# A hybrid attention and delta-rule layer on one core: TensorE's order written out through the merges

## The chip, the cores and the metric

The kernel runs on one core of a Trainium2 chip. The metric is device time of one launch in microseconds, the median of several runs. Besides, one execution was recorded by the hardware profiler; all traces below are of that kind.

## The reference, cut to what matters

One layer over 1024 latent tokens (16 rows of 64 columns) and 256 context tokens, width 1024, float32. Half of the mixing width is neighbourhood attention (8 heads of 64), the other half a bidirectional chunked gated DeltaNet (4 heads of 128), in chunks of which each needs the inverse of a unit lower triangular matrix.

```python
h = rmsnorm(x, g_pre) * (1 + scale) + shift;  hc = the same of ctx
na_q, na_k, na_v, na_z, g_qkv, g_z, g_b, g_a = split(h @ w_in)
o_na = neighborhood_attention(...)                # window 8 x 16, plus all context keys
q, k, v = gdn_qkv(g_qkv, conv_w)                  # centred conv, silu, l2norm, rotary
a = where(pos[:, None] > pos[None, :], (k * beta) @ k.T * decay, 0)
t_inv = triangular_solve(eye + a, eye)            # per chunk, head and direction
u = t_inv @ (v * beta);  w = t_inv @ (k * beta * exp(gc))
state, o = scan(...)                              # forward and backward over the chunks
y = concat([o_na * silu(na_z), rmsnorm(o_g) * silu(g_z)]) @ w_out
return x + gate * rmsnorm(y, g_post)
```

## The kernel before, in words

The kernel uses chunks of 128 tokens: 10 chunks (2 of context, 8 latent) for each of 4 heads and 2 directions, so 80 matrices `pm` of 128x128 whose inverses are needed. A float32 product of the projections is made of three products of rounded parts (`hh`, `hl` for the activations, `wh`, `wl` for the weights), in `mm_chan` and `mm_tok`.

Phases: `phase0` (modulation, first projections), `phase2` (projections, convolutions and the scan's front for the four heads, with other projections as filling), `phase_a2` (the last projections, the inverses, the loads for attention), `phase_b` (attention and scan by turns, then the output projection). In `phase_b` TensorE's order is written out: `pe(r)` orders each product behind the last one on the queue, without a semaphore. Before `phase_b` the order of every engine is set by Tile's scheduler, which gives the instructions of each engine an order from their place in the program, a priority (`tc.high_priority(offset)` moves instructions ahead by that many places) and a modelled time; the engines then run them in that order.

The projections left to `phase_a2` are those of the generator `projections`: two pairs of value tiles (264 columns a product), then queries, keys and gates of the attention pairs 2 and 3 (512 or 256 columns a product). A result in `pz` goes through ACT and DVE to `st_z` and by DMA to `z_dram` (line 557).

The inverses are built in two steps. `inv_groups`/`inv_blocks` invert the 320 diagonal blocks of 32x32 on DVE (lines 1078 and 1081), 120 blocks at a time; groups 0 and 1 are done in `phase2`, group 2 (80 blocks, tiles `ab_vv` and `tb_qh`) in `phase_a2` by the generator `blocks`, which then loads the masks and, when three heads are merged, the inputs of attention's pair 0 (`na_load`: `kk`, `qh`, `ql`, `gt`, `vv`). `inv_merge` then joins the blocks of one head into 64x64 and 128x128 inverses. It is a generator of stages, which `MERGES` calls by head and letter:
- l: load `pm` of the head into `pmf` and the inverted blocks into `vl`
- t: DVE transposes (lines 1114 to 1116) to `vd` and `ld`, ACT copies into `tm[0]`
- z: TensorE products `pm` by blocks (line 1128), ACT copies to `zt`; then ACT and POOL copies into `xo` and `tm[1]` (line 1137)
- u: TensorE (line 1147), DVE into `tm` and `xo` (line 1152)
- w: TensorE, the 64x64 level (line 1161), ACT copies to `z2`
- e: TensorE (lines 1167 and 1169), two halves of five chunks each in two PSUM buffers `tb`, DVE into `tm` (lines 1171 and 1172), DMA to `tm_dram` (line 1174)

`tm[0]` is one of two buffers by turns (`tms[h % 2]`), `tm[1]` is `tms[2]` for all heads, and so is `xo`. PSUM has three banks `ta`, two `tb` and three `pj` here. In `phase0`, `self.after` puts the first query product of one group of rows behind the last of the modulation's small products (line 310) on TensorE's queue. In `phase_a2` a step of the projections alternates with three steps of `blocks` and three of `merges`, all merge stages 200 places ahead. The scan's loads (`delta_load`: `tm`, `v`, `kt`, `kq`, `qe`, line 156) go to a pool that takes the memory of `wp` (weights, `st_z`) and `hp` (`hh`, `hl`). SP's queue issues nearly all DMAs, in one order; the weights' loads are on ACT's queue. In the scan, line 1232 (POOL) makes `kd` from `kt`, line 1260 (TensorE) is a step's first product here and line 1271 uses `kd`.

Of the kernel before, what the change touches and what calls it, by code (L numbers as in the profile page):

```python
# [11 lines left out]
F32 = mybir.dt.float32  # L12
# [125 lines left out]
MERGES = "0l 0t 1l 0z 0u 1t 0w 2l 0e 1z 1u 2t 1w 3l 1e 2z 2u 3t 2w 2e 3z 3u 3w 3e"  # L138
# [3 lines left out]
class K:  # L142
    def __init__(self, tc, I, out, dbg=None):
        self.tc, self.nc, self.I, self.out = tc, tc.nc, I, out
        self.dbg = dbg or {}
        self.na_first = None
        self.gm = {}
        self.gate = self.after = None
# [306 lines left out]
    def mm_chan(self, ps, w, hh, hl, t0, n, perm=False, ks=range(KC)):  # L455
        nc = self.nc
        his, los = w
        for k in ks:
# [4 lines left out]
            r = nc.tensor.matmul(ps, wh, xh, start=(k == 0), stop=False)  # L463
            if self.after:
                self.order(r, self.after)
                self.after = None
            nc.tensor.matmul(ps, wh, xl, start=False, stop=False)  # L467
            nc.tensor.matmul(ps, wl, xh, start=False, stop=(k == KC - 1))  # L468

    def mm_tok(self, ps, w, c0, n, xsel, ks=range(KC)):  # L470
        nc = self.nc
        his, los = w
        for k in ks:
            wh, wl = his[k][:, c0:c0 + n], los[k][:, c0:c0 + n]
            xh, xl = xsel(k)
            nc.tensor.matmul(ps, xh, wh, start=(k == 0), stop=False)  # L476
            nc.tensor.matmul(ps, xl, wh, start=False, stop=False)  # L477
            nc.tensor.matmul(ps, xh, wl, start=False, stop=(k == KC - 1))  # L478
# [610 lines left out]
    def inv_merge(self, g3, ps, h):  # L1089
        nc = self.nc  # L1090
        pm = []
        for d in range(2):
            pool, tag = (g3, f"pm{d}") if h % 2 else (self.pf, f"kk{d}")
            pm.append(pool.tile([P, 10, P], F32, name=f"pmf{h}_{d}", tag=tag))
            nc.sync.dma_start(pm[d][0:96], self.pm_dram[h][0:96, d])
        if h == 0:

            self.vls = [self.pf.tile([P, S], F32, name=f"vl{i}", tag=f"q{c}") for i, c in enumerate(("l0", "h1"))]
            self.tms = [g3.tile([P, 10, P], F32, name=f"tm{i}") for i in range(3)]
            self.xo = g3.tile([P, 10, 64], F32, name="xo")  # L1100
# [7 lines left out]

        xo = self.xo
        tm = [self.tms[h % 2], self.tms[2]]  # L1110
        yield
        vx = self.pf.tile([P, S], F32, name=f"vx{h}", tag="ql1")
# [10 lines left out]
        for d in range(2):  # L1123
            pz = ps.tile([P, 10, 32], F32, name=f"tz{h}_{d}", tag="ta", bufs=3)
            for t in range(10):
                for b in (0, 2):
                    s1, s2 = slice(32 * b, 32 * b + 32), slice(32 * b + 32, 32 * b + 64)
                    nc.tensor.matmul(pz[s2, t, :], pm[d][s1, t, s2], ld[s1, d, t, :], start=True, stop=True,
                                     tile_position=(32 * b, 32 * b + 32))
# [10 lines left out]
        for d in range(2):  # L1140
            pu = ps.tile([P, 10, 32], F32, name=f"tu{h}_{d}", tag="tb", bufs=2)
            where = [(r, r + c - 1) for r in (1, 3) for c in (0, 1) if (r, c) != ((3, 1), (1, 0))[d]]
            for t in range(10):
                for r, c in where:
                    s2, sc = slice(32 * r, 32 * r + 32), slice(32 * c, 32 * c + 32)
                    a, b = (zt, vd) if c < r else (vd, zt)
                    nc.tensor.matmul(pu[sc, t, :], a[s2, d, t, :], b[s2, d, t, :], start=True, stop=True,
# [9 lines left out]
        for d, t0, n in parts:  # L1157
            pz = ps.tile([P, 8, 64], F32, name=f"tz2{h}_{d}{t0}", tag="ta", bufs=3)
            for t in range(n):
                lo = xo[A, t0 + t, :] if d == 0 else tm[1][A, t0 + t, A]  # L1160
                nc.tensor.matmul(pz[B, t, :], pm[d][A, t0 + t, B], lo, start=True, stop=True, tile_position=(0, 64))
            nc.scalar.copy(z2[B, d, t0:t0 + n], pz[B, :n])
        yield
        for t0 in (0, 5):
            pus = [ps.tile([P, 8, 64], F32, name=f"tu2{h}_{d}{t0}", tag="tb", bufs=2) for d in range(2)]
            for t in range(5):
                nc.tensor.matmul(pus[0][A, t, :], z2[B, 0, t0 + t, :], tm[0][B, t0 + t, B], start=True, stop=True,
                                 tile_position=(64, 0))
                nc.tensor.matmul(pus[1][B, t, :], xo[B, t0 + t, :], z2[B, 1, t0 + t, :], start=True, stop=True,
# [270 lines left out]
    def phase_a2(self):  # L1440
        tc, ps = self.tc, self.ps
        with tc.tile_pool(name="a2", bufs=1, side="right", reuse_waits="tile") as ap:
# [13 lines left out]

            def merges():

                heads = [self.inv_merge(ap, ps, h) for h in range(4)]
# [10 lines left out]
            credit = [0.0, 0.0]  # L1470
# [86 lines left out]
```

## Time and profile before

| | us |
|---|---|
| median of 3 runs (lowest, highest) | 872.78 (872.28, 876.59) |
| the profiled execution: device time | 871.71 |
| its span in the trace | 869.9 |

What lies around the span is 1.8 us. Times in the trace run from the span's start. PE is TensorE's products, PEld its weight loads, DVE, ACT and POOL are VectorE, ScalarE and GpSimd, SPq is the queue of DMA issues on SyncE. A row of a timeline gives start, duration, engine, line, operation, output and inputs, shape and count, and in brackets how long the engine was idle before it and who released it. PEclk is the granted clock of TensorE as a share of full speed. Buffer numbers are left out of names: `tz` is the PSUM tile of stages z and w, `tu` that of u and e.

### The profile page before, as it was taken

To read this page: it belongs to the slowest core of one execution; us is meant where nothing else is said; L and a number is where in the kernel's file an instruction comes from. 1 tells how busy PE (TensorE), PEld (TensorE's weight loads), DVE (VectorE), ACT (ScalarE), POOL (GpSimd) and SP (SyncE) were. 2 spreads that over 40 slices of the span, in tenths; PEclk is the share of its full clock that TensorE was granted. 3 is DMA by queue.
4 is the path that set the end of the run, shared out by engine and by line. 5 is a ranking of instruction groups with operands and counts; after the bars stand their busy time and mean duration, and the time that the engine had idled before them with its cause. 6 is when DMAs were issued, how large, how long until landed. Compare 5 with 4: busy or idle time off the path is not lost.

```text
span 869.9 us, 16461 instructions
## 1 busy us (share of the span) xinstructions
PE 824.9 (95%) x6082; PEld 696.4 (80%) x6082; DVE 502.7 (58%) x1051; ACT 417.3 (48%) x1087; POOL 357.3 (41%) x430
## 2 busy tenths in 40 slices
PE   6999999999999989989898999899999999999996
PEld 3678887888788867769786788788898988878885
DVE  3444455536743699859935964456666655653342
ACT  5244334753664643355314334366666667734210
POOL 2224141453462553328262100655757559624110
PEclk9999999999999999989998999699999999999999
DMA  8778352255444825562597569995967925134251
GB/s 340 265 259 295 97 170 88 73 170 168 142 157 154 221 85 170 176 171 81 176 283 226 160 187 290 419 258 149 313 179 262 259 78 191 49 110 133 87 184 69
DMA packets 86054, 159.65 MB, mean 184 GB/s; under 512 B 18373, under 2 KB 45334, under 8 KB 83798
## 3 DMA queue, kind: packets, MB, share of 16 engines
q1 hardware_dynamic: 78486, 144.94, 53.0%
q10 hardware_dynamic: 7488, 13.67, 5.1%
q8 instruction: 48, 0.79, 0.4%
q14 instruction: 32, 0.26, 0.1%
HBM read 109.51 MB, written 52.42 MB: 186 GB/s over the span
## 4 chain that ended last, share of the span: by engine, by line
PE 59%; DVE 16%; DMA 15%; issue 4%; ACT 2%; POOL 2%; SPq 1%; DVEq 0%; POOLq 0%; ACTq 0%
PE py L1369 3%; PE py L1370 3%; PE py L1371 3%; DVE tb L1078 3%; DVE vb L1081 3%; PE pa L1260 2%; PE pz L463 2%; PE pz L468 2%; PE pz L467 2%; PE po L789 2%; DMA wada<-in_w_ada 2%; PE pa L1271 2%; PE po L784 2%; DMA pm_dram<-pm 2%; PE tr L772 2%
## 5 line engine op out<-in xcount | busy, mean ns | idle before, releaser
L759 ACT ACTIVATE pt<-pt,nm 128x544 f32<-128x544 f32 (+1 forms) x64 | 50.5, 790 | 37.5 <-DVE nm L758 37.0
L758 DVE CUSTOM_DVE_ANT_0 pt<-sc,gm 128x544 f32<-128x544 f32 (+1 forms) x64 | 49.4, 771 | 32.2 <-PE sc L754 25.8
L742 POOL TENSOR_TENSOR gm<-gt,mk 128x288 f32<-128x288 f32 (+1 forms) x48 | 46.5, 971 | 29.1 <-DVE nm L758 28.8
L1232 POOL TENSOR_SCALAR kd<-kt,kd 128x128 f32<-128x128 f32 x72 | 42.7, 605 | 20.5 <-PE pa L1271 19.9
L1020 ACT ACTIVATE em<-em,gc 128x128 f32<-128x128 f32 x80 | 25.5, 391 | 34.9 <-DMA em<-gc_dram 29.7
L467 PE MATMUL pz<-hl,wh_gz 128*128 128x512 f32 x96 | 38.6, 402 | 0.0
L463 PE MATMUL pz<-hh,wh_gz 128*128 128x512 f32 x96 | 38.3, 399 | 0.0
L468 PE MATMUL pz<-hh,wl_gz 128*128 128x512 f32 x96 | 38.2, 398 | 0.0
L476 PE MATMUL pv<-wh_nv,hh 128*128 128x264 f32 x128 | 35.5, 296 | 2.0 <-ACT hh L265 1.7
L477 PE MATMUL pv<-wh_nv,hl 128*128 128x264 f32 x128 | 36.8, 292 | 0.0
L1431 DVE TENSOR_TENSOR finv<-py,ggb 128x512 f32<-128x512 f32 x16 | 10.9, 689 | 43.2 <-ACT finv L1430 43.1
L478 PE MATMUL pv<-wl_nv,hh 128*128 128x264 f32 x128 | 35.6, 287 | 0.0
L1274 DVE SCALAR_TENSOR_TENSOR s<-s,egl,pa 128x128 f32<-128x128 f32 x64 | 19.6, 344 | 27.2 <-PE pa L1271 27.2
L1039 POOL TENSOR_SCALAR_AFFINE_SELECT qe<-qe 128x256 f32<-128x256 f32 x32 | 25.5, 800 | 24.1 <-DVE qe L1038 24.1
L887 DVE SCALAR_TENSOR_TENSOR acc_v<-xp_v,cols,acc_v 128x1282 f32<-128x1282 f32 x16 | 29.1, 1817 | 10.9 <-ACT acc_v L885 10.6
L1078 DVE TENSOR_TENSOR tb<-ab,vb 120x31 f32<-120x31 f32 (+15 forms) x62 | 30.2, 487 | 8.7 <-DMA ab<-ab_dram 7.1
L1137 POOL COPY tm<-ld 32x320 f32<-32x320 f32 x16 | 7.4, 464 | 65.0 <-DMA tm_dram<-tm 27.1
L1430 ACT ACTIVATE finv<-py 128x512 f32<-128x512 f32 x16 | 9.5, 597 | 48.6 <-PE py L1371 30.5
L1238 POOL TENSOR_SCALAR vb<-v,beta 128x128 f32<-128x128 f32 x40 | 24.2, 604 | 20.4 <-DVE y L1244 17.2
L772 PE MATMUL tr<-c,pt 128*96 128x128 f32 (+1 forms) x192 | 31.8, 275 | 0.0
L1035 DVE SCALAR_TENSOR_TENSOR pm<-pk,beta,em 128x128 f32<-128x128 f32 x80 | 23.5, 342 | 14.0 <-PE pk L1028 10.9
L770 ACT COPY tcx<-tc 128x256 f32<-128x256 f32 x64 | 23.4, 366 | 16.2 <-PE tc L768 15.8
(432 smaller groups left out, 2852.7 us busy)
## 6 DMA issues: line engine op xcount, KB each, us to landing
wada<-in_w_ada SPq DMA_DIRECT2D x16, 512.0 KB
em<-gc_dram SPq DMA_DIRECT2D x20, 256.0 KB
pm_dram<-pm SPq DMA_DIRECT2D x20, 256.0 KB
tm_dram<-tm SPq DMA_DIRECT2D x8, 640.0 KB
kk<-qk_dram SPq DMA_DIRECT2D x16, 320.0 KB
tm<-tm_dram SPq DMA_DIRECT2D x4, 1280.0 KB
kq_dram<-kq SPq DMA_DIRECT2D x4, 1152.0 KB
kq<-kq_dram SPq DMA_DIRECT2D x4, 1152.0 KB
```

Of the source, the lines that this page charges most:

```text
L463: r = nc.tensor.matmul(ps, wh, xh, start=(k == 0), stop=False)
L467: nc.tensor.matmul(ps, wh, xl, start=False, stop=False)
L468: nc.tensor.matmul(ps, wl, xh, start=False, stop=(k == KC - 1))
L476: nc.tensor.matmul(ps, xh, wh, start=(k == 0), stop=False)
L477: nc.tensor.matmul(ps, xl, wh, start=False, stop=False)
L478: nc.tensor.matmul(ps, xh, wl, start=False, stop=(k == KC - 1))
L742: r = nc.gpsimd.tensor_tensor(self.gm[hh][:, 384 - n:384].rearrange("p (n c r) -> p n c r", c=nco, r=4), gv, self.mk[:, mo:mo + n].rearran ...
L758: nc.vector.tensor_tensor_reduce(pt[:, 384 - n:], sc[:, 512 - n:768], gm[:, 384 - n:], -1.0, 3.0e38, ALU.add, ALU.min, nm)
L759: self.last_exp = nc.scalar.activation(pt[:, 384 - n:], pt[:, 384 - n:], AF.Exp, bias=nm, scale=-1.0, accum_out=sums[:, ct, hh:hh + 1]).in ...
L772: self.pe(nc.tensor.transpose(pl[:m, rc * P:(rc + 1) * P], pt[:, 384 + (rc - 3) * m:384 + (rc - 2) * m], self.ident))
L1078: nc.vector.tensor_tensor(t3, bc(ab[:, 0:m, m:m + 1], [r, m, n]), bc(vb[:, m:m + 1, m:], [r, m, n]), ALU.mult)
L1232: r = nc.gpsimd.tensor_scalar(kd[d], kt_[:, t, :], self.kd[:, h, d, t:t + 1], None, ALU.mult)
```

## The change

TensorE's order in `phase_a2` is written out. `mm` issues a product, chains it behind the last one with `pe` while `seq` is set, and counts the columns of products with 128 output rows, that is of the projections. When 120,000 columns of the stage are through, and after every 5,200 more, it calls `between`: three steps of `blocks` and one line of `MERGES`. A line holds one to three stages; the copies behind z have become a stage of their own, c. Head 0's stages l and t, and head 1's l, are issued before the projections, l and t with an offset of 600. All projections and merge products are one chain; nothing else of TensorE is in it.

Buffers: head 0's `vl` lies in `tms[2]`, which is zeroed again after the transposes, and its `vx` in the buffer of `z2`; `vl` of heads 1 and 2 in `ql0` and `qh1` of attention's pair 0, that of head 3 in head 1's; `pm` of head 1 in `kk0`, `kk1`, of heads 0 and 2 in two buffers of the stage's own (`pm0`, `pm1`), of head 3 in `vv` and in a buffer of `vd`. The blocks' loads now come ahead of `pm`'s in stage l. A manual order in `phase0` (`after`) is gone.

```diff
-MERGES = "0l 0t 1l 0z 0u 1t 0w 2l 0e 1z 1u 2t 1w 3l 1e 2z 2u 3t 2w 2e 3z 3u 3w 3e"
+MERGES = "0z 0c/0u 1t/0w 1z/0e 1c 2l/1u 2t/1w 2z/1e 2c 3l/2u 3t/2w 3z/2e 3c/3u/3w/3e"
+A2_FIRST, A2_NEXT = 120000, 5200
...
+    def mm(self, *a, **k):
+        r = self.nc.tensor.matmul(*a, **k)
+        if self.seq:
+            self.pe(r)
+        if self.between and a[0].shape[0] == P:
+            self.cols_left -= a[2].free_size()
+            if self.cols_left <= 0:
+                self.cols_left += A2_NEXT
+                between, self.between = self.between, None
+                between()
+                self.between = between
...
-            r = nc.tensor.matmul(ps, wh, xh, start=(k == 0), stop=False)
-            if self.after:
-                self.order(r, self.after)
-                self.after = None
-            nc.tensor.matmul(ps, wh, xl, start=False, stop=False)
-            nc.tensor.matmul(ps, wl, xh, start=False, stop=(k == KC - 1))
+            self.mm(ps, wh, xh, start=(k == 0), stop=False)
+            self.mm(ps, wh, xl, start=False, stop=False)
+            self.mm(ps, wl, xh, start=False, stop=(k == KC - 1))
...
     def inv_merge(self, g3, ps, h):
-        pm = []
-        for d in range(2):
-            pool, tag = (g3, f"pm{d}") if h % 2 else (self.pf, f"kk{d}")
-            pm.append(pool.tile([P, 10, P], F32, name=f"pmf{h}_{d}", tag=tag))
-            nc.sync.dma_start(pm[d][0:96], self.pm_dram[h][0:96, d])
         if h == 0:
-            self.vls = [self.pf.tile([P, S], F32, name=f"vl{i}", tag=f"q{c}") for i, c in enumerate(("l0", "h1"))]
...
-            for w in (*self.vls, *self.tms, self.xo):
+            for w in (self.tms[2], *self.tms[:2], self.xo):
                 nc.gpsimd.memset(w, 0.0)
-        vl = self.vls[h % 2]
+            self.vls = [self.tms[2].rearrange("p t c -> p (t c)")[:, :S]]
+        elif h < 3:
+            self.vls.append(self.pf.tile([P, S], F32, name=f"vl{h}", tag=("ql0", "qh1")[h - 1]))
+            nc.gpsimd.memset(self.vls[h], 0.0)
+        else:
+            self.vls.append(self.vls[1])
+        vl = self.vls[h]
...
+        if h < 3:
+            pieces = [(d, 0, (self.pf.tile([P, 10, P], F32, name=f"pmf{h}_{d}", tag=f"kk{d}") if h == 1 else
+                              g3.tile([P, 10, P], F32, name=f"pmf{h}_{d}", tag=f"pm{d}", bufs=1))) for d in range(2)]
+        else:
+            w = self.pf.tile([P, 2 * S], F32, name="pmf3", tag="vv").rearrange("p (t c) -> p t c", c=P)
+            pieces = [(0, 0, w[:, :10]), (1, 0, w[:, 10:15]),
+                      (1, 5, g3.tile([P, 5, P], F32, name="pmf3_1", tag="vd", bufs=2))]
...
         nc.vector.transpose(vx, vl)
+        if h == 0:
+            nc.gpsimd.memset(self.tms[2], 0.0)
...
                 nc.scalar.copy(zt[s2, d], pz[s2])
+        yield
         for b in range(4):
...
     def phase_a2(self):
             def merges():
-                for c in MERGES.split():
-                    h = int(c[0])
-                    while c[1:] == "l" and (8 * h + 7) // 12 not in self.yd:
-                        yield
-                    next(heads[h])
-                    if c[1:] == "e":
-                        ready.append(h)
+                for line in MERGES.split("/"):
+                    for c in line.split():
+                        with tc.high_priority(offset=200):
+                            stage(c)
                     yield
-            pr, gens = self.fill, (blocks(), merges())
...
+            with tc.high_priority(offset=600):
+                stage("0l")
+            with tc.high_priority(offset=300):
+                next(blocks)
+            with tc.high_priority(offset=600):
+                stage("0t")
+            stage("1l")
+            self.lines, self.cols_left = merges(), A2_FIRST
+            self.last_pe, self.seq = None, True
+            def between():
+                for _ in range(3):
+                    next(blocks, None)
+                next(self.lines, None)
+            self.between = between
+            for _ in self.fill:
+                pass
+            self.between = None
+            for _ in self.lines:
+                pass
+            self.seq = False
+            for _ in blocks:
+                pass
```

More of the change, by code (lines that the diff above doesn't have):

```diff
@@ L147, in __init__ @@
         self.gm = {}
-        self.gate = self.after = None
+        self.gate = self.last_pe = self.last_hh = None
+        self.seq, self.between = False, None
     def order(self, r, before):
@@ L1470, in phase_a2 @@
-            credit = [0.0, 0.0]
-            first = True
-            for _ in range(3):
-                next(pr)
-            for _ in pr:
-                for i, (g, r) in enumerate(zip(gens, (3, 3))):
-                    credit[i] += r
-                    while credit[i] > 0:
-                        if i:
-                            with tc.high_priority(offset=200):
-                                next(g, None)
-                        elif first:
-                            first = False
-                            with tc.high_priority(offset=300):
-                                next(g, None)
-                        else:
-                            next(g, None)
-                        credit[i] -= 1
@@ L1488, in phase_a2, with stage @@
-            for g in gens:
-                for _ in g:
-                    pass
+            heads = [self.inv_merge(ap, ps, h) for h in range(4)]
+            blocks = blocks()
+            def stage(c):
+                next(heads[int(c[0])])
+                if c[1:] == "e":
+                    ready.append(int(c[0]))
+            def merges():
+                for line in MERGES.split("/"):
+                    for c in line.split():
+                        with tc.high_priority(offset=200):
+                            stage(c)
+                    yield
```

24 lines of the change are left out of this document (14 added, 10 removed).

## The prediction

> **What bounds the kernel now.** I read the page first: busy shares, then the slices.
>
> ```profile
> span 869.9 us, 16461 instructions
> PE 824.9 (95%) x6082; PEld 696.4 (80%) x6082; DVE 502.7 (58%) x1051; ACT 417.3 (48%) x1087; POOL 357.3 (41%) x430
> PEclk9999999999999999989998999699999999999999
> ```
>
> TensorE is the bound, busy 95% of 869.9 us. The granted clock is full except in a few slices; the worst one (6 tenths, the 26th of 40, around 544 to 565 us) is where this stage ends. So I cut the stage into stretches with the windows view. Columns: length, then busy time (instructions) of PE, weight loads, DVE, ACT, POOL, then clock, DMA share, GB/s.
>
> ```profile
> 425.90:464.90 39.00, 39.00 (x187) 32.43 (x186) 17.77 (x52) 6.25 (x11) 17.42 (x22) 1.00 0.90 262
> 464.90:469.60 4.70, 1.53 (x8) 0.68 (x6) 4.20 (x7) 2.16 (x5) 0.02 (x1) 1.00 0.94 282
> 469.60:492.00 22.40, 22.40 (x323) 18.58 (x325) 19.75 (x36) 12.43 (x26) 7.00 (x8) 0.85 0.50 154
> 492.00:495.30 3.30, 1.21 (x69) 1.09 (x68) 3.15 (x8) 1.25 (x3) 0.00 (x0) 1.00 0.67 215
> 495.30:515.30 20.00, 19.96 (x242) 16.57 (x242) 14.17 (x38) 6.82 (x16) 1.95 (x4) 0.91 0.61 202
> 515.30:522.00 6.70, 6.70 (x140) 5.52 (x140) 3.52 (x5) 2.77 (x7) 0.00 (x0) 1.00 0.91 209
> 534.10:552.40 18.30, 15.17 (x341) 13.93 (x341) 7.00 (x14) 6.52 (x16) 5.38 (x10) 0.70 0.97 341
> 552.40:560.00 7.60, 6.66 (x34) 5.98 (x34) 3.10 (x9) 3.69 (x10) 5.79 (x9) 0.60 1.01 421
> ```
>
> Two kinds of loss are to be seen: idle time (length minus PE busy) and half clock (busy time times one minus the clock). Idle: 4.70-1.53 = 3.2, 3.30-1.21 = 2.1, 18.30-15.17 = 3.1, together 8.4 us. Clock: 22.4x0.15 = 3.4, 20.0x0.09 = 1.8, 15.2x0.30 = 4.6, together 9.8 us. So 18.2 us are lost between 464.9 and 552.4. Who ends these waits, from the timeline of PE (start, duration, engine, line, operation, what it waited for):
>
> ```profile
> 469.57 0.62 PE L1128 MATMUL tz<-ld,pmf 32*32 32x32 f32 x20 [1.61 <-DVE ld L1116]
> 495.34 0.79 PE L1167 MATMUL tu<-tm,z 64*64 64x64 f32 x10 [2.13 <-DVE tm L1171]
> 530.35 0.39 PE L463 MATMUL pz<-hh,wh_gz 128*128 128x512 f32 x1
> 531.95 0.40 PE L467 MATMUL pz<-hl,wh_gz 128*128 128x512 f32 x1
> 533.58 0.51 PE L468 MATMUL pz<-hh,wl_gz 128*128 128x512 f32 x1
> 552.38 0.58 PE L751 MATMUL sc<-kk,qh 128*128 128x256 f32 x1
> 559.27 0.61 PE L1271 MATMUL pa<-vn,kd 128*128 128x128 f32 x4
> ```
>
> Head 0's first merge product waits for its transposed input. The last projection product ends at 534.1, and from there to the first scores at 552.4 TensorE has only what is left of the merges of heads 2 and 3, each stage waiting for the copies of the one before. That tail has no cover.
>
> **The change, part by part.** Arithmetic and bytes of the projections and merges stay. The fill: products of 512 columns follow each other every (531.95-530.35)/7 = 0.229 us. Of the 185,088 columns left to the stage, 25,344 are the value products, over by 425.9. The first turn comes after 120,000, so 94,656 columns or 42.4 us later, plus what the last scan front takes between:
>
> ```profile
> 425.90:464.90 39.00, 3.94 (x16) 3.04 (x16) 1.00 0.90 262
> 425.90:464.90 39.00, 1.20 (x8) 0.91 (x8) 1.00 0.90 262
> ```
>
> That is 5.1 us (lines 1030 and 944 alone), so head 0's first product stands at about 473.5, 4 us later than now. Its input has been started earlier, at higher priority. So the first loss goes: -3.2 idle and -3.4 clock. Each later turn is 5200/512x0.229 = 2.3 us behind the stage before, twelve times, and the thirteenth (the last stage of head 3) leaves 2,688 columns, 1.2 us. So the tail gets cover: -3.1 and -4.6; the loss at 492 to 515 goes too (-2.1, -1.8) as far as nothing below replaces it. Sum: -18.2.
>
> What the written order adds. Stage lengths and the waits inside them, from the timelines of PE, DVE, SP's queue, ACT and POOL (the second row is line 1147 alone, in the windows view):
>
> ```profile
> 516.63 1.45 PE L1128 MATMUL tz<-ld,pmf 32*32 32x32 f32 x80
> 525.00:528.00 3.00, 1.46 (x120) 1.35 (x120) 1.00 1.02 316
> 485.41 1.38 PE L1161 MATMUL tz<-xo,pmf 64*64 64x64 f32 x20
> 519.14 0.79 PE L1167 MATMUL tu<-tm,z 64*64 64x64 f32 x10
> 494.81 0.47 DVE L1171 TENSOR_SCALAR tm<-tu 64x320 f32<-64x320 f32 x1
> 495.31 0.49 DVE L1172 TENSOR_SCALAR tm<-tu 64x320 f32<-64x320 f32 x1
> 497.73 0.84 SPq L1174 DMA_DIRECT2D tm_dram<-tm  x2
> 501.12 1.86 ACT L1120 COPY tm<-vd 32x320 f32<-32x320 f32 x4 [0.67 <-DMA tm_dram<-tm]
> 523.94 0.49 DVE L1172 TENSOR_SCALAR tm<-tu 64x320 f32<-64x320 f32 x1
> 532.11 1.96 POOL L1137 COPY tm<-ld 32x320 f32<-32x320 f32 x4 [27.12 <-DMA tm_dram<-tm]
> ```
>
> Stage z is 1.4 us, u 1.4 (line 1147's share of 525 to 528), w two times 1.35 and e four times 0.72 (1.38 and 0.79 less the overlap with what follows).
> - Inside e: its two halves use the same two PSUM buffers, and nothing may stand between them now. The second needs two DVE operations (0.47+0.49) and some 0.1 us of hand-over (494.81+0.47 to the product at 495.34): 1.1 us, four heads, +4.4. Bounds: 2.3 (0.57 each, if only the first of the two operations counts) and 8.5 (2.13 each, as at 495.34).
> - From e to the next head's w: the shared buffer `tms[2]` must be in DRAM before the next head writes it. e's last DVE operation ends 1.0 us after e; the store took 3.4 us for head 0's (issued at 497.7, seen by ACT at 501.1) and 7.7 for head 1's (524.4 to POOL at 532.1, with the DMA busy); two of the four POOL copies are 1.0 more: ready 5.4 to 9.7 us after e. The second half of w stands 2.3+1.4+2.3+1.35 = 7.4 us after e. Wait 0 to 2.3 us, three times: 0 to 6.9. I take +3.0: none for head 1, where traffic is as light as at 498, 1.5 for each of the two later ones.
> - Transposes of heads 1 to 3, zeroing of buffers, the moved stores of pair 0's inputs: they lie on DVE, POOL (idle over half of this stage) and SP under TensorE's products, +0. Pair 0's `kk` comes free with head 1's w, not head 2's as now, so its loads come earlier: no term either, but room on the DMA.
> - Clock inside the stage: 0, as in the row 515.30:522.00, where the same mixture without idle time ran at 1.00. The other end is the 0.85 of 469.60:492.00, 3.4 us for one fall, 6.8 for two.
>
> - The order that goes out of `phase0` put six query products behind the modulation's last small products (line 310), ahead of a wait:
>
> ```profile
> 50.13 0.95 PE L310 MATMUL pa<-c,rows 128*128 128x2 f32 x8
> 53.55 0.75 PE L476 MATMUL pv<-wh_nv,hh 128*128 128x264 f32 x4 [0.94 <-ACT hh L265]
> ```
>
> Without it six key products of the same length can stand there: 0; bounds -0.9 (the wait gone) and +1.4 (six times 0.229 uncovered).
>
> So the stage would end at 552.4-18.2+7.4 = 541.6.
>
> Then a cost behind it. The projections now end there too, and they hold what the scan's loads overwrite.
>
> ```profile
> 536.82 0.54 SPq L557 DMA_DIRECT2D z_dram<-st_z  x1
> 539.74 0.90 SPq L156 DMA_DIRECT2D tm<-tm_dram  x1
> 543.14 0.32 SPq L156 DMA_DIRECT2D kt<-kt_dram  x1
> SPq L156 <- DMA z_dram<-st_z: 1.3, 1, 1.3
> 552.46 1.21 POOL L1232 TENSOR_SCALAR kd<-kt,kd 128x128 f32<-128x128 f32 x2 [0.45 <-DMA kt<-kt_dram]
> ```
>
> Today the last projection ends at 534.1, its result is stored from 536.8, `kt` may only be loaded when that store has landed (543.1) and arrives at 552.5, 18.3 us after the projection, under 421 GB/s of other loads. The scan uses it at 559.3, 6.9 us after the stage's end, so it is hidden. In the new order it is not: bounded below by today's 2.7 us to the store and 3.4 us (the light store at 498) for it and for the load, 9.5; above by today's 18.3. I take 10, since pair 0's loads are out of the way by then. With POOL's 1.2 us the scan's product comes at 11.2 instead of 6.9: +4.3 (bounds +3.8 and +12.6).
>
> Sum: -18.2+4.4+3.0+4.3 = -6.5. The profiled execution was 871.7 us with a span of 869.9; that gives 865.2, and against the median of three, 872.8 (1.1 above that execution), 866.3.
>
> **The rivals.**
> *The clock halves at every e.* TensorE then idles 1.1 us in each e among 64x64 products, and at 492 an idle of 2.1 us among such was followed by a stretch at 0.91. One fall costs 3.4 us (469.60:492.00); two cancel the gain, four give 866.3+13.6 = 879.9: slower. Against it: 515.30:522.00 at 1.00. The Trainium skill, TensorE: Matmul & The Clock Gate, section A second HAM failure mode: psum-queue depth-cycling, speaks for this rival: it says that TensorE idling briefly between groups while PSUM buffers are cycled makes the clock swing between half and full. The trace agrees at 492 and not at 515. Chance 0.13.
> *The scan's loads take as long as now*, 18.3 us behind the projections: +12.6 in place of +4.3, so 874.6, no change. For it: the DMA share of 0.97 before 552. Against: pair 0's loads come earlier. Break-even is `kt` 16.5 us behind the projections' end. Chance 0.14.
> *Head 3 waits for the last block inverse.* DVE shows when that is done now (first and last operation, then the next users):
>
> ```profile
> 462.51 0.20 DVE L1078 TENSOR_TENSOR tb_qh<-ab_vv 80x31 f32<-80x31 f32 x1 [11.92 <-DMA ab_vv<-ab_dram]
> 510.51 0.19 DVE L1081 TENSOR_TENSOR ab_vv<-ab_vv,tb_qh 80x31 f32<-80x31 f32 x1
> 523.09 0.83 DVE L1116 STREAM_TRANSPOSE ld<-vd 128x640 f32<-128x640 f32 x1
> ```
>
> Head 3's input is ready at 523.9, 13.2 us after the inverse. The written order wants it in the ninth turn: 473.5, plus eight fills (18.6), plus 26 us of stages before it by the lengths and waits above: 518. If the inverse ends as late as now, TensorE waits 6 us: 872.3, no change, or 876 with a fall of the clock. Against: its load has fewer transfers ahead (one head's, not two), and DVE stood idle for the 11.9 us before it. Chance 0.16.
> *More is gained*: no wait for `tms[2]` (-3.0), and the start of attention and scan, today 6.66 us of products at clock 0.60 (552.40:560.00), at full clock (-2.7): 860.6. Against it: the wait for `kt` leaves TensorE idle just there. Chance 0.12. That the order isn't followed is excluded by its being a chain; that it changes nothing would need the tail's 7.7 us to be hidden today, which the chain of PE rows above denies.
>
> **How the numbers follow.** The forecast has 0.45. About 0.5% (4.4 us) is what a measurement can tell here. Faster by more: 0.40 of the forecast's 0.45, and 0.12: 0.52. Slower: 0.11 of the clock's 0.13, 0.03 of the loads', 0.03 of the inverse's: 0.17. The rest, 0.31, within. Predicted 866.3; its own range, from the bounds of e (-2.1, +4.1) and w (-3.0, +3.9), 861 to 874; with the rivals 859 to 878.
>
> **What would show it.** In the changed kernel: no wait before the first L1128 product, which comes near 473; clock 1.00 from there to the stage's end; about 1.1 us between the halves of e; a wait of 1 to 2 us in the w of heads 2 and 3; scores beginning near 542; then a wait of some 4 us before the scan's first products, ended by `kt`. It is wrong if the clock row of that stretch is under 0.92, if head 3's first product waits for its transpose, or if `kt` lands over 16 us behind the last projection product.

## The result, and the profile after

The changed kernel takes 893.97 us (median of 4, 889.88 to 896.47), the kernel before, run beside it, 872.53 (870.51 to 876.59). The ratio is 1.0246, with a 95% interval of 1.0208 to 1.0284: 21 us slower, where 6 us faster was forecast. The profiled executions have spans of 893.8 and 869.9 us.

From the page of the changed kernel:

```profile
span 893.8 us, 16470 instructions
PE 830.7 (93%) x6082; PEld 700.7 (78%) x6082; DVE 510.1 (57%) x1051; ACT 417.8 (47%) x1087; POOL 359.2 (40%) x431
PEclk9989999999999989999999698799999999999999
```

TensorE is busy 5.8 us longer than before (830.7 against 824.9, from the page shown in the prediction) with the same 6082 instructions, so its products ran at half clock for longer (the mean granted clock is 0.962, before 0.972); the other 18 us of the difference are idle time. To place them I cut both executions at four products: the last value product, the first scores, the first `kd` product of the scan and the last scores. The windows view of the kernel before (length, busy time of PE, weight loads, DVE, ACT, POOL, then clock, DMA share, GB/s):

```profile
0.00:424.70 424.70, 403.95 (x2231) 332.21 (x2232) 257.19 (x420) 207.40 (x507) 164.83 (x168) 0.98 0.53 171
424.70:552.40 127.70, 119.27 (x1486) 99.43 (x1484) 76.70 (x169) 43.10 (x91) 34.75 (x49) 0.92 0.79 244
552.40:559.30 6.90, 5.96 (x28) 5.28 (x28) 2.79 (x7) 2.98 (x9) 5.25 (x8) 0.55 1.01 422
559.30:763.00 203.70, 197.68 (x1878) 180.73 (x1877) 124.33 (x388) 136.08 (x417) 129.88 (x177) 1.00 0.67 198
```

and of the changed kernel:

```profile
0.00:431.40 431.40, 408.12 (x2232) 337.26 (x2233) 259.89 (x422) 207.67 (x507) 164.43 (x168) 0.97 0.52 169
431.40:565.40 134.00, 119.74 (x1486) 98.70 (x1485) 79.38 (x167) 42.33 (x90) 32.38 (x44) 0.91 0.70 204
565.40:580.90 15.50, 6.17 (x27) 4.31 (x25) 2.99 (x7) 5.10 (x13) 7.98 (x13) 0.63 0.98 379
580.90:787.00 206.10, 198.60 (x1877) 181.74 (x1877) 126.18 (x388) 135.12 (x414) 131.23 (x178) 0.99 0.67 199
```

Four losses: 6.7 us before any merge begins (431.4-424.7), 6.3 in the stage of the merges (134.0-127.7), 8.6 between the first scores and the scan's first `kd` product (15.5-6.9), 2.4 in the scan; 24.0 of the 23.9 us between the spans. Inside the stage TensorE's idle time rose from 127.70-119.27 = 8.4 to 134.00-119.74 = 14.3 us. It was to fall to about what the written order adds, 7.4. By the prediction's measure, busy time times one minus the clock, the stage lost 119.27x0.08 = 9.5 us to half clock before and loses 119.74x0.09 = 10.8 now, where none was to be left. The waits of TensorE between 460 and 600 us in the changed kernel (total, times, longest); line 160 is the helper `mm`, through which all projections and merge products go, 1182 VectorE's copies behind u, 1201 and 1202 those behind e:

```profile
PE pa L1290 <- DMA v<-vt_dram: 7.0, 1, 7.0
PE tz L160 <- DVE xo L1182: 4.5, 1, 4.5
PE tu L160 <- issue: 3.6, 1, 3.6
PE tu L160 <- DVE tm L1201: 3.1, 4, 1.4
PE sc L765 <- DVE nm L772: 2.0, 1, 2.0
PE pq L160 <- DVE sl_k L543: 1.9, 1, 1.9
PE tu L160 <- DVE tm L1202: 1.2, 4, 0.3
```

All but the first, which is the scan's, and the 2.0 of the scores lie in the stage and add up to its 14.3 us. The 3.6 us stand inside head 2's stage u; nothing that the profile shows ends them, and their cause stays open. The wait of 4.5 us is the first w, of head 0, and the prediction had not listed it. The timeline of the changed kernel around it (rows of VectorE, TensorE and GpSimd in turn):

```profile
485.60 1.37 DVE L1095 TENSOR_TENSOR ab_vv<-ab_vv,tb_qh 80x247 f32<-80x247 f32 x1
487.00 0.42 DVE L1092 TENSOR_TENSOR tb_qh<-ab_vv 80x252 f32<-80x252 f32 x1
...
489.75 1.51 DVE L1095 TENSOR_TENSOR ab_vv<-ab_vv,tb_qh 80x256 f32<-80x256 f32 x1
...
492.65 0.42 DVE L1095 TENSOR_TENSOR ab_vv<-ab_vv,tb_qh 80x252 f32<-80x252 f32 x1
492.99 0.47 DVE L1182 TENSOR_SCALAR tm<-tu 32x320 f32<-32x320 f32 x1
494.01 1.24 PE L160 MATMUL tz<-xo,pmf 64*64 64x64 f32 x12 [4.50 <-DVE xo L1182]
485.26 1.44 POOL L466 TENSOR_TENSOR wl_gz<-wr_gz,wh_gz 128x512 fp32r<-128x512 f32 x1 [4.99 <-ACT wh_gz L465]
489.71 1.26 POOL L466 TENSOR_TENSOR wl_gz<-wr_gz,wh_gz 128x512 fp32r<-128x512 f32 x1 [3.02 <-ACT wh_gz L465]
```

Stage u of head 0 left TensorE at about 487. The copies of it that w needs (line 1182) begin only at 492.99, because VectorE works its queue in order and from 487.0 on ten operations of the last block inverse, and one of a projection, stand there first. TensorE's order was written, VectorE's was not: it is still placed by the compiler's model. Two of the inverse's operations in these rows take 1.4 to 1.5 us where their like takes 0.42, each beside an operation of GpSimd (485.26 to 486.70, 489.71 to 490.97). The Trainium skill, SBUF — State Buffer, section SBUF: two separate sides, has a rule for it: VectorE and GpSimd share a pair of ports as an exclusive lock, so that an operation with two SBUF inputs waits for one of GpSimd that reads SBUF. The trace agrees twice in these rows. Behind the wait the clock is at half from 494.4 to 504.6:

```profile
496.00:500.00 4.00, 4.00 (x90) 3.88 (x90) 3.90 (x7) 2.61 (x7) 0.00 (x0) 0.50 0.75 157
```

If that fall is this wait's doing, it cost some 5 us more, an estimate: half of 10.2. It is not in this run alone: p0, eta and abfirst, further down, wait 4.6 to 4.7 us at the same w, and there the clock is at half for 13.7 us.

The first wait of the list is that of the scan:

```profile
565.17 0.39 PE L160 MATMUL pz<-hh,wl_gz 128*128 128x512 f32 x1
566.94 0.32 SPq L571 DMA_DIRECT2D z_dram<-st_z  x1
569.49 0.42 SPq L173 DMA_DIRECT2D v<-vt_dram  x1
570.24 0.32 SPq L173 DMA_DIRECT2D kt<-kt_dram  x1
578.17 0.77 PE L1290 MATMUL pa<-v,tm 128*128 128x128 f32 x2 [6.99 <-DMA v<-vt_dram]
```

The last projection product is at 565.17, right ahead of the scores; `v` and `kt` are issued 4 to 5 us later, and `v` lands at 578, with the DMA engines 0.98 busy (the row 565.40:580.90). The stage's end and the projections' end are now one point, and everything that waits for the projections' buffers starts there.

### The profile page after: what moved, and what is told of

The parts are those of the page before. It is cut to its first block, busy times and chain, and to the rows that moved or that the text cites. A ratio compares the mean times of both kernels' runs of the same rounds, so it can differ in the third digit from the quotient of the medians.

```text
span 893.8 us, 16470 instructions
## 1 busy us (share of the span) xinstructions
PE 830.7 (93%) x6082; PEld 700.7 (78%) x6082; DVE 510.1 (57%) x1051; ACT 417.8 (47%) x1087; POOL 359.2 (40%) x431
## 4 chain that ended last, share of the span: by engine, by line
PE 61%; DVE 19%; DMA 10%; issue 4%; ACT 3%; POOL 2%; SPq 1%; ACTq 0%; DVEq 0%; POOLq 0%
PE pz L160 6%; PE pv L160 4%; PE gpl_k L160 4%; PE gpl_q L160 4%; DVE tb L1092 3%; PE py L1399 3%; DVE vb L1095 3%; PE py L1400 3%; PE py L1401 3%; PE pk L160 3%; PE pa L1290 3%; DMA pm_dram<-pm 2%; PE pa L1301 2%; PE po L803 2%; PE po L798 2%
## 5 line engine op out<-in xcount | busy, mean ns | idle before, releaser
L1053 POOL TENSOR_SCALAR_AFFINE_SELECT qe<-qe 128x256 f32<-128x256 f32 x32 | 25.5, 801 | 23.7 <-DVE qe L1052 23.3
L160 PEld LDWEIGHTS pv<-wh_nv,hh 128*128 128x128 f32 x128 | 25.4, 208 | 8.0 <-ACT hh L282 5.3
```

The lines of the kernel that those rows point to most:

```text
L160: r = self.nc.tensor.matmul(*a, **k)
```

## The experiments

Every run has the boundaries of the tables above. "Link" is the ordering link of phase 0, which the change took out. All medians are in us; the kernel before, run on the same chip in each group of runs, had medians of 872.3 to 873.2. The last three columns are of the one profiled execution, whose own time is the third column: for b_nop0, bufs and eta_mid it is 6 to 8 us above the median, for later 4 below.

| run | median | profiled | ratio to before, 95% | last value product | from it to the scores | from the scores to `kd` |
|---|---|---|---|---|---|---|
| before | 872.53 | 871.71 | | 424.7 | 127.7 | 6.9 |
| the change | 893.97 | 895.67 | 1.0246 (1.0208-1.0284) | 431.4 | 134.0 | 15.5 |
| p0: link back | 890.49 | 893.06 | 1.0202 (1.0174-1.0230) | 427.3 | 135.9 | 15.7 |
| b_nop0: before without the link | 878.44 | 884.75 | 1.0078 (1.0047-1.0109) | 431.5 | 132.2 | 7.4 |
| nochain: p0, no written order | 886.71 | 886.63 | 1.0172 (1.0150-1.0194) | 424.8 | 140.8 | 7.5 |
| bufs: before with the moved buffers | 872.62 | 879.24 | 1.0019 (0.9998-1.0041) | 424.8 | 130.3 | 7.4 |
| eta: p0, e in the group of three | 885.82 | 884.74 | 1.0159 (1.0137-1.0182) | 423.3 | 126.2 | 17.1 |
| abfirst: p0, inverse's load called first | 887.89 | 887.89 | 1.0178 (1.0149-1.0207) | 423.6 | 133.9 | 15.3 |
| later: p0, first turn at 140800 | 888.95 | 884.80 | 1.0190 (1.0161-1.0218) | 424.5 | 140.7 | 7.3 |
| eta_mid: eta, first turn at 130400 | 881.19 | 888.70 | 1.0111 (1.0076-1.0146) | 427.7 | 131.3 | 13.8 |
| eta_later: eta, first turn at 140800 | 878.83 | 879.26 | 1.0070 (1.0045-1.0095) | 425.1 | 132.8 | 7.5 |
| next78: eta, turns of 7800 | 880.60 | 880.17 | 1.0105 (1.0089-1.0122) | 425.0 | 134.3 | 7.5 |
| sa_later: eta_later, stores on ACT | 880.34 | 880.86 | 1.0093 (1.0078-1.0109) | 423.1 | 138.3 | 7.2 |
| sa_next78: next78, stores on ACT | 883.47 | 885.61 | 1.0136 (1.0117-1.0156) | 427.3 | 138.3 | 7.8 |
| h3_later: eta_later, head 3's own buffer | 873.75 | 874.36 | 1.0018 (1.0005-1.0032) | 425.0 | 128.1 | 7.2 |
| h3_ab: h3_later, inverse's load called first | 873.65 | 873.64 | 1.0016 (0.9996-1.0037) | 424.1 | 126.7 | 8.3 |
| h3_next: h3_later, turns of 6500 from 130400 | 869.17 | 869.17 | 0.9959 (0.9944-0.9974) | 425.3 | 122.0 | 7.8 |

### The link of phase 0

p0 puts the link back into the changed kernel with these lines in `mm`, and a flag `in_chan` that is set around the first product of `mm_chan`; b_nop0 takes the link out of the kernel before:

```diff
+        if self.after and a[0].shape[0] == P and self.in_chan:
+            self.order(r, self.after)
+            self.after = None
```

> The changed kernel with one part taken back: the ordering link in phase 0 (a first channel product stands behind a named instruction of TensorE) is there again, the written order of the merges stays. Theory 1: the link's removal cost 3.5 us at the first group's end (93.4 to 97.1 us from the span's start) and about 3 more until the value products end (425.3 to 431.7); then this one takes 887 to 890.5 us, against 894.0 with the link removed, and the first group's last product is back at 93 to 94. Rival: the shift has another cause (instructions placed otherwise because the merges are emitted otherwise), and the time stays at 892 to 896 with the group's end at 97.

> The kernel before with only the phase 0 ordering link taken out. Theory 1: 872.5 plus 3.5 to 6.6 us, 876 to 879, with the first group's end at 97. Rival (the link does nothing by itself): 870 to 874 and 93.4.

b_nop0 is 0.5 to 1.1% slower than before, 6.0 us by the medians, by this link alone. Its timeline and one window:

```profile
52.40 0.40 PE L465 MATMUL pk<-hh,wqk_l 128*128 128x512 f32 x1
52.63 0.95 PE L310 MATMUL pa<-c,rows 128*128 128x2 f32 x8
55.58 1.25 PE L473 MATMUL pv<-wh_nv,hh 128*128 128x264 f32 x4 [2.00 <-ACT hh L265]
50.00:60.00 10.00, 8.00 (x41) 7.07 (x40) 3.58 (x7) 5.88 (x10) 1.28 (x2) 0.83 0.91 317
```

With the link the eight small products of the modulation ran at 50.13 and six query products filled the time until `hh` came (wait 0.94, the prediction's rows). Without it the compiler puts query and key products first, the small ones come 2.5 us later, and nothing is left to fill: 2.00 us of waiting, and then the clock falls (0.83 in that window; full before). The group's last query product is at 97.7 in place of 93.4, and the value products end at 431.5 as in the changed kernel (431.4), in an execution that is 6.3 us above its median. In the changed kernel the link's return gave 3.5 us by the medians, at the edge of what was expected and with intervals that overlap; its profiled start (427.3) is among the latest of the runs that have the link (423.1 to 427.7). Theory 1 holds by b_nop0, and its size is 4 to 9.5 us by that run's interval.

### The written order, and the moved buffers

nochain takes out the two lines that chain TensorE's instructions; bufs is the kernel before with the changed `inv_merge` alone.

```diff
         r = self.nc.tensor.matmul(*a, **k)
-        if self.seq:
-            self.pe(r)
```

> As the run with the phase 0 link put back, and the written order of TensorE is taken off: stages are emitted at the same column counts, with the same buffers and loads, but nothing holds TensorE's instructions in the order of emission. Theory 2: it is the fixed order that makes TensorE stand at the first merges (1.9 us at the first z product, 4.5 at head 0's w, 3.6 before u) while projections are ready behind it; without it projections fill these, the stage ends 5 to 12 us earlier and the time is 876 to 884 us. Rival A: the inputs are late because of the moved buffers and the later load of the block inverse, so the stage ends at the same place and the time stays at 886 to 891. Rival B: without the order the merges come out even later than they do with it, and the time is 892 or more.

> The kernel before (its rule of turns between blocks, merges and projections, TensorE's order left to the compiler, the phase 0 link in place) with the changed kernel's merge buffers alone: where vl, pm and vx lie, and the extra clearing of the third tm buffer. Theory 4a: the moved buffers cost the 13 us that the run without the written order lost between the value products' end and the first scores; then this one takes 880 to 887. Rival 4b: the buffers are harmless, it is the emission at fixed column counts that loses them; then 870 to 875.

From the windows of nochain and of p0, in that order:

```profile
424.80:565.60 140.80, 129.55 (x1484) 106.60 (x1483) 79.64 (x169) 43.06 (x91) 36.09 (x51) 0.86 0.74 227
565.60:573.10 7.50, 6.55 (x27) 5.81 (x27) 2.79 (x7) 3.50 (x9) 5.17 (x8) 0.51 0.97 336
```

```profile
427.30:563.20 135.90, 122.98 (x1485) 101.29 (x1484) 79.21 (x169) 42.31 (x90) 32.32 (x45) 0.87 0.71 205
563.20:578.90 15.70, 7.12 (x28) 5.50 (x26) 2.98 (x7) 5.18 (x13) 8.00 (x13) 0.61 0.99 375
```

My theory 2 falls as it was put: without the order the merges' stage is not 5 to 12 us shorter but 4.9 longer, in the one execution of each that was profiled. That nochain is the faster of these two has 2.5 us ahead of the stage (424.8 against 427.3), and more behind it: the compiler lets the projections end ahead of the last merges (536.4, the scores at 565.6), the loads run beside these, and 8.2 us come back (15.7 to 7.5). By the medians it is 3.8 us faster, with intervals that overlap. The moved buffers, the rival's cause, cost nothing that can be told (bufs, 1.0019). So the written order does shorten the stage against the same emission without it, and loses more behind it. What in the emission at column counts makes nochain's stage 13 us longer than the 127.7 of before was not settled.

### The two halves of e

```diff
-    tag="tb", bufs=2
+    tag="ta" if t0 else "tb", bufs=3 if t0 else 2
```

> As the run with the phase 0 link put back, and the second half of every merge's stage e takes its PSUM buffers from the group of three (tag ta) in place of the group of two, so its products need not wait for VectorE to empty the first half's. The trace showed 0.86 us of waiting per e, 3.4 over four. Theory: 2.5 to 3.5 us less than the run with the link put back (2 more if the clock falls at 526 and 536 us go with it). Rival: the wait only moves to the next product that needs the half's result, and the time is the same within 0.5 us.

```profile
423.30:549.50 126.20, 116.16 (x1485) 96.16 (x1483) 79.17 (x168) 42.46 (x91) 32.52 (x46) 0.91 0.73 215
549.50:566.60 17.10, 5.68 (x27) 4.06 (x27) 2.99 (x7) 5.04 (x13) 7.77 (x13) 0.74 0.98 363
```

4.7 us by the medians, with intervals that overlap, and expected were 2.5 to 3.5, or 2 more with the clock; in the two profiled stages 9.7 (135.9 to 126.2), with busy time down 6.8 at a clock of 0.91 in place of 0.87. That the small waits draw half clock after them is seen best by place. The list above has waits of 0.6 to 1.4 us on line 1201, which end at 506.2, 524.4, 547.2 and 562.8. Within 2 us behind the first three the clock falls to half, for 3.4 us each (from 508.0, 525.2 and 549.0); these windows hold the last 2.4 or 2.5 us of each stretch and the full clock behind it:

```profile
509.00:512.40 3.40, 3.40 (x69) 2.46 (x70) 3.06 (x12) 0.99 (x3) 0.00 (x0) 0.64 0.96 386
526.10:529.50 3.40, 3.40 (x13) 2.61 (x10) 0.98 (x2) 0.91 (x2) 0.00 (x0) 0.64 1.04 239
550.00:553.40 3.40, 3.40 (x82) 2.44 (x83) 0.00 (x0) 0.00 (x0) 0.00 (x0) 0.64 0.90 363
```

In eta the e's have no such wait; they end at 497.7, 514.9, 535.1 and 547.8, and the clock falls behind none of them within 5 us. Its stretches at half clock (482.6 to 496.4, 510.0 to 513.4, 520.2 to 527.0) stand at or behind other waits, of 4.7, 1.1 and 2.7 us.

This stage of eta is 1.5 us shorter than that of the kernel before, and the kernel is still 1.6% slower: the 17.1 us from the scores to `kd` hold 10.2 of it. That is theory 3.

### Where the projections end

```diff
-A2_FIRST, A2_NEXT = 120000, 5200
+A2_FIRST, A2_NEXT = 140800, 5200
```

> As the run with the phase 0 link put back (890.5 us), and the first line of merges stands behind 140800 columns of the projections in place of 120000, so the last four lines stand behind the last projection. Theory 3: what costs behind the stage is that the projections end with it, and the scan's loads (queued behind the last projection's store) land 15.7 us after the stage's end, against 6.9 before the change. Here the projections end about 12 to 16 us ahead of the stage's end and the loads land beside the merges: the gap between the stage's first scores and the first kd product falls from 15.7 to 7 or 8 us, and the wait of 4.7 at head 0's w shrinks. The last lines stand uncovered and cost 3 to 6 us of waits; sum 880 to 886. Rival: the uncovered merges cost as much as the loads gain, with the clock at half through them, and the time is 889 or more.

> As the run with the second half of stage e in the group of three PSUM buffers (885.8 us), and the first line of merges behind 140800 columns. Theory 3: the gap between the first scores and the first kd product falls from 17.1 us to 7 or 8; the uncovered last lines cost 3 to 5 us; 876 to 882. Rival (uncovered merges eat the gain): 885 or more.

> As the run before this one with 130400 columns, two lines of merges behind the last projection. Theory 3: about half of the scan loads' delay goes (4 to 5 us), the uncovered lines (3w, 3e) cost 2 to 3: 880 to 884. Rival: no better than 885.8.

With four lines of merges behind the last projection the gap is 7.3 and 7.5 us, as theory 3 said; with two it is still 13.8. For later alone the rival's total came true: of the gap's 8.4 us the uncovered lines eat 4.8 (stage 140.7), and the median is 888.95, 1.5 below p0. Without e's waits 7.0 us remain of it (885.8 to 878.8).

### What holds the merges now: VectorE's queue, the turns, the store

abfirst moves `next(blocks)` ahead of `stage("0l")`; next78 has 120000 and 7800; the stores' edit is

```diff
-        for d in range(2):
-            nc.sync.dma_start(self.tm_dram[h][:, d], tm[d])
+        for d in (1, 0):
+            nc.scalar.dma_start(self.tm_dram[h][:, d], tm[d])
```

> As the run with the phase 0 link put back (890.5 us), and the load of the last block-inverse group is issued ahead of the first merge's loads, so the block inverse starts earlier on VectorE (before the change its load was issued at 451.3 us and its first operation stood at 462.5; with the link put back 459.4 and 467.6). Theory 2b: the 4.7 us wait at head 0's w is u's evacuation queued on VectorE behind some 17 block-inverse operations; with 4 to 6 us of head start it shrinks by 2 to 5 us, the stage ends so much earlier, and the time is 885.5 to 888.5. Rival: VectorE's order is placed by the model, which puts the same number of operations ahead whenever the load comes; the wait stays at 4 to 5 and the time at 889 to 892.

> As the run with 140800 columns and the group of three PSUM buffers (878.8 us), but the four lines behind the last projection come from longer turns: the first line of merges stands behind 120000 columns and each next behind 7800 (it was 5200), so every stage has about 3.25 us of projections in front of it in place of 2.2. Theory 2: what a stage waits for (u's evacuation for w, 7.0 us in four waits; the store of tm for the next head's w, 7.5 us in one) arrives a fixed time after the stage before, so 1.1 us more per line takes 4 to 7 us of these waits, and the time is 872 to 876. Rival: the waits are set by VectorE's queue and by the store's landing, which shift with the merges, and the time stays at 877 to 880.

> As the run with 140800 columns and the group of three PSUM buffers (878.8 us), but the stores of a merged head (tm to DRAM) are issued from ScalarE's queue, the second direction first. In that run the next head's w stood 7.5 us for the single third tm buffer: its store was issued at 508.3 and the copy into it came at 516.3, with the DMA engines 0.85 to 1.01 busy with the attention's loads ahead of it in SP's queue. Theory: on its own queue the store lands in 3 to 4 us, the waits at the w of heads 1 and 3 shrink by 5 to 9 us together, and the time is 871 to 875. Rival: the 16 DMA engines are the limit, whatever queue issues; the landing still takes 6 to 8 us and the time stays at 877 to 880.

> Both of the edits before: turns of 7800 columns and the tm stores on ScalarE's queue. If both theories hold, 868 to 873, the same as the kernel before or a little under it. If the store's landing is what both remove, no better than the better of the two.

abfirst did not make the head start that it was meant to make. These are the issues of the inverse's load in p0 and in abfirst:

```profile
459.40 0.42 SPq L1074 DMA_DIRECT2D ab_vv<-ab_dram  x1
454.95 0.42 SPq L1074 DMA_DIRECT2D ab_vv<-ab_dram  x1
```

That is 32 and 31 us behind the last value product (427.3 and 423.6), behind the same transfers on SP's queue, and in both runs the same 36 operations of the inverse stand on VectorE ahead of the first copy that w needs; the wait stays at 4.6 us. So theory 2b was not tested: that a shorter queue on VectorE removes this wait is read from the trace and not shown by a run. As the order is the same, the 2.6 us between the two medians are what runs on different chips can differ by.

Longer turns (880.6 against 878.8) and the other queue (880.3) gave nothing; both rivals held within 0.6 us, and the two together were slower (883.5). The timeline of eta_later shows why: GpSimd's copy into `tms[2]` waits for the previous head's store out of it.

```profile
507.46 0.84 SPq L1209 DMA_DIRECT2D tm_dram<-tm  x2
516.32 1.96 POOL L1172 COPY tm<-ld 32x320 f32<-32x320 f32 x4 [35.99 <-DMA tm_dram<-tm]
542.20 1.56 SPq L1209 DMA_DIRECT2D tm_dram<-tm  x2
551.62 1.96 POOL L1172 COPY tm<-ld 32x320 f32<-32x320 f32 x4 [16.75 <-DMA tm_dram<-tm]
552.62 2.07 PE L160 MATMUL tz<-tm,pmf 64*64 64x64 f32 x17 [7.52 <-POOL tm L1172]
```

The store is seen 8.9 and 9.4 us after its issue. The long wait is that of 3w, behind the store of head 2, and not 1w's as I had written in what was expected of the run with the stores on ScalarE. From ScalarE's queue it was no sooner:

```profile
506.52 0.90 ACTq L1209 DMA_DIRECT2D tm_dram<-tm  x2
515.24 1.96 POOL L1172 COPY tm<-ld 32x320 f32<-32x320 f32 x4 [36.71 <-DMA tm_dram<-tm]
542.21 0.33 ACTq L1209 DMA_DIRECT2D tm_dram<-tm  x1
555.10 1.96 POOL L1172 COPY tm<-ld 32x320 f32<-32x320 f32 x4 [21.31 <-DMA tm_dram<-tm]
```

TensorE's wait in 3w was 9.7 us in this run. The two issues of a store are 1.3 MB (2 x 640 KB). In the 3.4 us of the kernel before, the DMA engines moved 383 GB/s, 1.3 MB in all, no more than the store. In the 8.9 and 9.4 us of eta_later they moved 319 and 343 GB/s, 2.8 and 3.2 MB, and in the 12.9 us here 372, 4.8 MB, with a DMA share of 0.97 to 1.01 in all of these. So it is the DMA engines that are full, at 542 with the scan's loads that theory 3 brought there, and not the queue. What can be taken away is the dependence:

```diff
+        if h == 3:
+            tm[1] = g3.tile([P, 10, P], F32, name="tm3", tag="pm1", bufs=1)
+            nc.gpsimd.memset(tm[1], 0.0)
```

> As the run with 140800 columns and the group of three PSUM buffers (878.8 us); head 3's second direction is merged in the buffer that held head 2's second merge matrix (free once 2w is done), cleared on GpSimd, in place of the third tm buffer, which head 2's store still reads. In that run 3w stood 7.5 us for a copy into that buffer, the store being issued at 542.2 and landing at 551.6. Theory 5: this wait goes (6 to 8 us, 1 more of the clock), the time is 870 to 873. Rival: VectorE's and ScalarE's copies or the scan's loads are as late, and the time is 876 or more.

> As the run before with the last block inverse's load also issued first. If the 2.6 us that this gave with 120000 columns hold here too, 868 to 870; if it was only the shorter queue ahead of head 0's w, which stands 8 us later here, 870 to 873, the same.

> As the run with head 3's own buffer, and turns of 6500 columns from 130400 on, so that the projections end at the same line. Longer turns gave nothing when the store was the wait (880.6 against 878.8); if that store hid them, 1 to 3 us better than the run with head 3's own buffer; otherwise the same within 1 us or up to 2 worse.

The wait at 3w goes, and 5.1 us with it (878.8 to 873.8; 0.8 above the range expected). h3_ab has the order of h3_later on SP's queue, as abfirst had that of p0, and the same time (873.7). And now longer turns give 4.6 us (6500 columns, where next78 had 7800; 6500 without head 3's buffer was not run): 869.17, 0.4% faster than the kernel before (interval 0.26 to 0.56%) and 24.8 us under the changed one. Its longest waits between 425 and 556:

```profile
PE tz L160 <- DVE xo L1190: 3.2, 1, 3.2
PE pq L160 <- DVE sl_k L548: 1.5, 1, 1.5
PE sc L770 <- DVE tm L1210: 1.0, 1, 1.0
```

## Why the prediction was wrong, by its own steps

- *The link of phase 0, taken as 0 (bounds -0.9 and +1.4).* It measured 6.0 us (b_nop0). The step argued that key products could stand where the query products had stood. It looked at the filling and not at what the link puts early: the small products that `hh` waits for. The upper bound priced six products and left out that the wait and the half clock behind it come with them.
- *The losses of 18.2 us go.* The places of the losses were right, and the order cures them only where its inputs are ready. Of the changed stage 14.3 us are idle (forecast: 7.4). Head 0's first product came at 481.4, not 473.5; 6.7 of these 7.9 us are the late start. Then the first w stood 4.5 us for a cause not on the list, VectorE's queue. The term of +0, work that lies on VectorE "under TensorE's products", is a step that failed: it counted how much of the stage VectorE was idle, and not the order in its queue. The 3.6 us in head 2's u were on no list either, and their cause stays open.
- *Clock inside the stage, 0 (one fall 3.4, two 6.8).* The largest term that failed. The 9.8 us of half clock were to go; by the same measure the stage loses 10.8, about 5 of it behind the first w and the rest behind three e's and the wait of 3.6 us. The stage was forecast at 541.6-424.7 = 116.9 us and took 134.0: of these 17.1 us, 6.9 are idle time (14.3 against 7.4), and the clock is the greater part of the rest. That "the same mixture without idle time ran at 1.00" was a true reading, but the new order was not without idle time.
- *e, +4.4.* In waiting right: 3.1 and 1.2 us, 4.3. In effect too small, since the clock was put at 0. The first sign named as fatal is there: the clock from the first merge product to the scores is 0.86, under 0.92. The rival of the clock halving at every e, given 0.13, took place at three e's, for 3.4 us each, so that a fall cost 1.7 us there and not the 3.4 that it was priced at. The Trainium skill, TensorE: Matmul & The Clock Gate, section A second HAM failure mode: psum-queue depth-cycling, names just such brief idling between groups, and the trace now agrees at 509, 526 and 550.
- *w and the store, +3.0.* In the changed kernel's list this wait does not show. It was 2.1 us in p0, 1.1 in eta and 7.5 in eta_later, where the scan's loads run beside the merges; why the changed kernel is free of it was not tested.
- *The scan's loads, +4.3 (bounds 3.8 and 12.6).* Right in mechanism, and it measured 8.6: `v` and not `kt` ended the wait. "Pair 0's loads are out of the way by then" was the reason for the low value; the DMA share there was 0.98.
- *Head 3 waiting for the last inverse* (rival) did not happen: no wait of that kind is in the list.

With the sizes measured for the link (+6.0), the stage (134.0 in place of 127.7, +6.3), the scan's start (+8.6) and the scan (+2.4) the sum is +23.3, against 21.4 between the medians. Against the forecast of -6.5 the profiled spans are 30.4 us off: 6.7 ahead of the merges, 17.1 in the stage, 4.3 more than allowed at the scan's start and 2.4 in the scan, whose cause was not looked for. What share of the stage's loss is the clock and what the waits themselves is read from the traces and was not separated by an experiment of its own; filling the idle time with other products was not tried.

## What to carry to other kernels

An order written out for one engine is only as good as the queues that feed it: before fixing TensorE's order, follow each input to the engine that makes it and read that engine's order, not its share of busy time. Where work is spread over a long stage until its very end, look for what starts at that end; here loads that had been hidden for 18 us came into the open, and letting the projections end four lines of merges earlier closed that gap by 8 us. And a cure can seem worthless while another wait hides it: turns of 7800 columns gave nothing while a store was waited for, turns of 6500 gave 4.6 us once the last head had a buffer of its own. Last, an edit in the program is not yet a change in the queues: two runs that called a load earlier left it where it was.

## What the runs showed of the hardware

Waits of 0.6 to 1.4 us among 64x64 products were followed by half clock at three of four places in the changed kernel, and without them (eta) the clock fell behind none of the four. The Trainium skill, TensorE: Matmul & The Clock Gate, section HAM oscillation — how this bites in real kernels, names idle gaps over about 3.4 us as the danger, and here shorter ones were enough. A store's time from issue to landing went with the traffic beside it and not with its queue: 3.4 us when 1.3 MB moved in that time, as much as the store holds, 8.9 to 9.4 us from SP's queue with 2.8 to 3.2 MB, 8.7 to 12.9 from ScalarE's with 2.5 to 4.8 MB.
